# Retention loop of a decoder step: rows fetched a head ahead, rotary products after the values, states on other queues, x chunks one ahead

## The chip, the core and the metric

The kernel runs on one core of a Trainium2 chip. The core has five engines with queues of their own: TensorE (PE, with its weight loads shown apart as PEld), VectorE (DVE), ScalarE (ACT), GpSimd (POOL) and SyncE (SP). An engine takes the instructions of its queue in order; an instruction that has to wait holds up what stands behind it. Transfers between the chip's memory (DRAM) and the on-chip SBUF are issued from the queues of SP, ACT or POOL. The metric is device time in microseconds; lower is better.

## The reference, cut to what matters

One layer of a decoder: half-step SwiGLU, a token mixer of two branches (spatial gating and multi-scale retention), and a second half-step SwiGLU, on 512 prompt tokens and 8 x 8 new tokens (576 columns in all). The change touches the retention branch and the preparation of its input. Per head (8 heads, 128 wide queries and keys, 256 wide values):

```python
def rotary(x, pos):                       # angle per position and per one of 64 frequencies
    x1, x2 = xf[..., :half], xf[..., half:]
    return concatenate([x1 * cos - x2 * sin, x1 * sin + x2 * cos], axis=-1)

def retention_chunk(q, k, v, S, log_gamma):
    scores = einsum('blhd,bshd->bhls', q, k) * decay[None]
    intra = einsum('bhls,bshe->blhe', scores, v)
    inter = einsum('blhd,bhde->blhe', q, S) * q_decay[None, :, :, None]
    S_new = exp(L * log_gamma) * S + einsum('blhd,blhe->bhde', k * k_decay, v)
    return intra + inter, S_new
```

For the prompt the state starts at zero and runs through four chunks of 128 tokens; for the new tokens a state of 128 x 256 for each of 8 sequences and 8 heads is read, used and written back. The result is normalised per head, multiplied with a gate and goes through the projection w_b, whose products are summed over the heads.

## The kernel before, in words

Activations lie transposed in SBUF: 128 channels on the partitions, the 576 tokens along the row, so that "a row" or "a chunk" below is a tile of 128 x 576 in fp32 (288 KB). Each matrix product is made of three products of values split into a high and a low part (hi and lo), so that each weight tile and each operand is cast by ACT (`ACT.copy` to hi) and subtracted by DVE (lo): L150 and L151 for weights, L158 and L159 in `split`.

The program is traced in one order by Python; the tile framework then places the instructions of each engine's queue, also out of the traced order where an instruction isn't ready by its own estimate. Work that should run beside the matrix products is written as generators: `start(gen, delay)` hands one over, each `tick(us)` after some matmuls takes time off its delay and runs it to its next `yield`, and `finish` runs it to its end.

**The stages around the change.** The first FFN ends at about 460 us. Then 21 pairs of projections (q and k per head, gate rows, sigmoid gates) stream through `stream(pair2(w))` (L1236), whose results go to DRAM by POOL's queue (L1129): `qkd` holds q and k of each head, `rgd` the two gate rows of each head. Beside it, the generator `operands_of_values` (L1208) brings the residual x back from DRAM (`x1d`) in eight chunks of 128 channels: it issues the load of a chunk (POOL, L1215), yields for 6 us of ticks, multiplies it with the norm's row (DVE, L1217), shifts and scales it (ACT L1219, DVE L1223), and splits it into X (ACT L1225, DVE L1227). Tiles of 128 x 576 there come from a pool of `SSLOT` = 11 slots.

Then the loop over the heads (L1503 to L1517) begins. Its tiles come from a pool of `NSLOT` = 33 slots, made by `mix_pools` (L1244) after the first 24 matmuls of head 0's values, which also loads the rotary table `rope` and the constants `selI`. Per head:

- `fetch(hd)` (L1266): six loads of the q and the k row on SP: the row itself (L1272, x) and a second copy whose halves change places (L1273 and L1274, y: partitions 64 to 127 to 0 to 63 and back); two loads of gate rows (L1278); then two products on DVE (x with the cosines L1280, y with the signed sines L1281) and a sum on POOL (L1282).
- `values_of(hd)` (L1285): loads of w_in (SP, L139), 4 x 24 matmuls L1295 and 16 matmuls L1308 for the new tokens; copies out of PSUM on ACT (L1301).
- `out_b(hd - 2)` (L1486), twice: w_b's loads, 16 products of 6 matmuls (L447) with their copies on ACT (L1492), and eight stores to `accd`, for head 0 plain stores on SP (L1496), then accumulating stores on POOL (L1498).
- `finish(prev)`, and `core(hd)` (L1317) is started; it runs in pieces beside the values and out_b of the next turn.

For head 0 the values come before the fetch. `core` loads the head's constants `hc` (SP L1321) and the states `S0` of the new tokens in four loads of 256 KB (SP L1325; four buffers, so a load waits for the store of the head before to land), makes the scores (PE L1331, L1338, DVE L1333, L1340), transposes k (L1355, L1369; ACT L1357, L1371), corrects the low parts (DVE L1377, L1381), makes the four prompt states S (PE L1393, DVE L1396 and L1398; store of the last on SP, L1402), the product with S0 (PE L1409), the outputs (L1422 to L1443), the new states (PE L1452, DVE L1456; four stores on SP, L1457), the norm (PE L1467, ACT L1471, DVE L1474 to L1482, POOL L1481) and the split for out_b (`split`).

PSUM has eight banks, all from one pool (`bank()`), so a product that needs a bank waits until some engine has read an older one.

Of the kernel before, what the change touches and what calls it, by code (L numbers as in the profile page):

```python
# [28 lines left out]
EPS = 1e-6  # L29
NT = 5  # L30
SG = 4
NSLOT = 33
NSLOT2 = 7
SSLOT = 11
FSLOT = 12
# [44 lines left out]
def layer_kernel(ctx: ExitStack, tc: tile.TileContext, a):  # L80
# [5 lines left out]
    pp = ctx.enter_context(tc.tile_pool(name="pp", bufs=8, space=PSUM))  # L86
    dr = ctx.enter_context(tc.tile_pool(name="dr", bufs=1, space=DRAM))
    wp = ctx.enter_context(tc.tile_pool(name="wp", bufs=1))
    snp = ctx.enter_context(tc.tile_pool(name="snp", bufs=1))
    places = ExitStack()  # L90

    count = [0]
# [10 lines left out]
        return stack.enter_context(tc.tile_pool(name=nm(name), bufs=1, side=side, reuse_waits="tile"))  # L103

    now["xa"], now["xs1"] = pool(places, "xa"), pool(places, "xs1")

    def slot(shape, dt=F32):

# [23 lines left out]
    def whl(shape):  # L132
        small = len(shape) == 3 and shape[1] == 1
        tag = "whs" if small else "whl"
        return wp.tile([P] + shape, F32R, tag=tag, name=nm(tag), bufs=1 if small else 4)

    def load_raw(src, k0, kc, c0, cols):
        raw = raw4([kc, cols])
# [479 lines left out]

    def snap(ps, t=None):
        if t is None:  # L620
            t = snp.tile([P, H], F32, tag="sn", name=nm("sn"), bufs=3)
        ACT.copy(out=t, in_=ps[:, :H])  # L622
        return t

# [583 lines left out]
    def operands_of_values():  # L1208

        g = a2()  # L1210
        row = slot([P, T])
        POOL.dma_start(out=row, in_=rowd)
        for c in range(KC):
            t = slot([P, T])
            POOL.dma_start(out=t, in_=x1d[:, c])  # L1215
            yield 6.0
            DVE.tensor_tensor(out=t, in0=t, in1=row, op=ALU.mult)  # L1217
# [47 lines left out]

    def fetch(hd):  # L1266

        rope, t = tks["rope"], []
        for i in range(2):
            src = qkd[:, 2 * hd + i]  # L1270
            x, y = slot([P, T]), slot([P, T])
            nc.sync.dma_start(out=x, in_=src)  # L1272
            nc.sync.dma_start(out=y[0:64], in_=src[64:128])  # L1273
            nc.sync.dma_start(out=y[64:128], in_=src[0:64])  # L1274
            t.append((x, y))
        rg = [slot([P, T]) for _ in range(2)]
        for e in range(2):
            nc.sync.dma_start(out=rg[e], in_=rgd[:, 2 * hd + e])  # L1278
        for x, y in t:
            DVE.tensor_tensor(out=x, in0=x, in1=rope[:, 0], op=ALU.mult)  # L1280
            DVE.tensor_tensor(out=y, in0=y, in1=rope[:, 1], op=ALU.mult)  # L1281
            POOL.tensor_tensor(out=x, in0=x, in1=y, op=ALU.add)  # L1282
        return t[0][0], t[1][0], rg

    def values_of(hd):  # L1285
        wv = [load_w(win, 4 * i, 4, RV0 + hd * DV, DV) for i in range(2)]
        rv = []
        for n in range(4):
            ps = bank()
            i = 0  # L1290
            for kk in range(KC):
                wh, wl = (w[:, kk % 4, :] for w in wv[kk // 4])
                xh, xl = (x[:, n * P:(n + 1) * P] for x in X[kk])
                for s, m in ((xh, wh), (xl, wh), (xh, wl)):
                    PE.matmul(ps[:, :DV], lhsT=s, rhs=m, start=i == 0, stop=i == 23)  # L1295
                    i += 1
            if not rts:
                mix_pools()
            if n % 2 == 0:
                rv.append(slot([P, 2, DV]))  # L1300
            ACT.copy(out=rv[n // 2][:, n % 2, :], in_=ps[:, :DV])  # L1301
            tick(24 * 0.109)
        rvs = rts[0].tile([P, DV], F32, tag="rvs", name=nm("rvs"), bufs=2)
        ps = bank()
        i = 0
        for kk in range(KC):
            for w in wv[kk // 4]:
                PE.matmul(ps[:, :DV], lhsT=tks["hs"][:, kk, :], rhs=w[:, kk % 4, :], start=i == 0, stop=i == 15)  # L1308
                i += 1
        sw = half()  # L1310
        ACT.copy(out=sw[0:NS, :DV], in_=ps[NS:P, :DV])
        ACT.copy(out=sw[NS:P, :DV], in_=ps[0:NS, :DV])
        DVE.tensor_tensor(out=rvs, in0=ps[:, :DV], in1=sw[:, :DV], op=ALU.add)
        tick(16 * 0.109)
        return rv, rvs

    def core(hd, q, k, rg, rv, rvs, OB):  # L1317
        rt, selI = rts
        qdS = tks["qdS"]
        hc = rt.tile([P, 338], F32, tag="hc", name=nm("hc"), bufs=2)  # L1320
        nc.sync.dma_start(out=hc, in_=a["hconst"][hd])  # L1321
        S0 = []
        for j in range(4):
            t = rt.tile([P, 2, DV], F32, tag="S0", name=nm("S0"), bufs=4)
            nc.sync.dma_start(out=t, in_=a["state_ret"][0, 2 * j:2 * j + 2, hd].rearrange("b d e -> d b e"))  # L1325
            S0.append(t)

        ps = bank()
        for n in range(4):
# [61 lines left out]
        for n in range(4):  # L1391
# [7 lines left out]
                    out=t, in0=S[-1], scalar=lg[hd] ** P, in1=ps[:, :DV], op0=ALU.mult, op1=ALU.add  # L1399
                )  # L1400
            S.append(t)
        nc.sync.dma_start(out=a["ret_state_prompt"][0, 0, hd], in_=S[3])  # L1402
        yield 4.0

        pi = bank()
# [43 lines left out]
        for j in range(4):  # L1449
            ps = bank()  # L1450
            for i in range(2):
# [5 lines left out]
            nc.sync.dma_start(  # L1457
                out=a["ret_state_sample"][0, 2 * j:2 * j + 2, hd].rearrange("b d e -> d b e"), in_=S0[j]
            )
        yield 4.0  # L1460
# [19 lines left out]
        for e in range(2):  # L1480
            POOL.tensor_tensor(out=o[e], in0=o[e], in1=rg[e], op=ALU.mult)  # L1481
            DVE.tensor_tensor(out=o[e], in0=o[e], in1=r, op=ALU.mult)  # L1482
            split(OB[e][0], OB[e][1], o[e])
        yield 0.0

    def out_b(hd, OB, j):  # L1486
        wb = load_w(a["w_b"][0], 2 * hd, 2, j * 512, 512)
        for c in range(4):
# [4 lines left out]
                tick(cost(2))  # L1493
            dst = accd[:, 4 * j + c, :]
            if hd == 0:
                nc.sync.dma_start(out=dst, in_=t)  # L1496
            else:
                POOL.dma_start(out=dst, in_=t, accum_op=ALU.add)  # L1498


    prev = None
    OBs = []
    for hd in range(HEADS):  # L1503
        if hd == 0:
            rv, rvs = values_of(hd)
            q, k, gates = fetch(hd)
        else:
            q, k, gates = fetch(hd)
            rv, rvs = values_of(hd)
        if hd > 1:  # L1510
            for j in range(2):
                out_b(hd - 2, OBs[hd - 2], j)
        if prev:
            finish(prev)
        OBs.append([])
        prev = core(hd, q, k, gates, rv, rvs, OBs[hd])
        start(prev, 0.5)  # L1517


# [204 lines left out]
        xt2.append(xp.tile([P, 2, T], F32, tag="x", name=nm("x2"), bufs=4))  # L1724
        nc.sync.dma_start(out=xt2[p], in_=x1d[:, 2 * p:2 * p + 2, :])
    xs = [xt2[c // 2][:, c % 2] for c in range(KC)]
    now["xs1"] = pool(ffn2, "xs1")
    now["wraw"] = pool(ffn2, "raw")
    ops.clear()
    now["hl"] = pool(hreg, "hl", "right")  # L1730
# [118 lines left out]
def shape_constants():  # L1849
# [5 lines left out]
    ang = (pos[None, :] * inv[:, None]).astype(f32).astype(np.float64)  # L1855
    rope = np.zeros((P, 2, T), f32)
    rope[0:64, 0], rope[64:128, 0] = np.cos(ang), np.cos(ang)
    rope[0:64, 1], rope[64:128, 1] = -np.sin(ang), np.sin(ang)
    hconst = np.zeros((HEADS, P, 338), f32)
    i = np.arange(P)  # L1860
    j = np.arange(NS)
# [54 lines left out]
```

## Time and profile before

| | us |
|---|---|
| median of three runs | 1746.78 (1738.07 to 1747.7) |
| the profiled execution | 1745.23 |
| its span, first to last instruction | 1743.5 |
| PE busy | 1667.8 (96%) |
| DVE busy | 1132.4 (65%) |
| ACT busy | 789.9 (45%) |
| POOL busy | 276.3 (16%) |
| mean granted PE clock | 0.982 of full |

How to read the rows quoted below. In the timeline a row has start, length, engine, line of the kernel, operation, the tile written and the tiles read, shapes, and how many instructions were merged; in brackets stands how long the engine had been idle before and what released it. "SPq" and "ACTq" are the queues that issue transfers; their instructions do not count as busy. In the table of waits: who waited on which line for whom, total us, times, longest. In the table of stretches: busy time of each engine with the number of instructions, the granted PE clock (1.00 is full), the mean busy share of the 16 DMA engines and the GB/s they moved. In the answers for one line: shortest, median and longest duration in ns, then the starts of the first and the last.

### The profile page before, as it was taken

To read this page: it belongs to the slowest core of one execution; us is meant where nothing else is said; L and a number is where in the kernel's file an instruction comes from. 1 tells how busy PE (TensorE), PEld (TensorE's weight loads), DVE (VectorE), ACT (ScalarE), POOL (GpSimd) and SP (SyncE) were. 2 spreads that over 40 slices of the span, in tenths; PEclk is the share of its full clock that TensorE was granted. 3 is DMA by queue.
4 is the path that set the end of the run, shared out by engine and by line. 5 is a ranking of instruction groups with operands and counts; after the bars stand their busy time and mean duration, and the time that the engine had idled before them with its cause. 6 is when DMAs were issued, how large, how long until landed. Compare 5 with 4: busy or idle time off the path is not lost.

```text
span 1743.5 us, 30978 instructions
## 1 busy us (share of the span) xinstructions
PE 1667.8 (96%) x12324; PEld 1588.9 (91%) x12324; DVE 1132.4 (65%) x1796; ACT 789.9 (45%) x1374; POOL 276.3 (16%) x340
## 2 busy tenths in 40 slices
PE   8999999999999999997988889999999999999997
PEld 4889999999999988987978889889999999999997
DVE  6857847676787766736654556355656958676773
ACT  5533525344655546533444444523335625344454
POOL 0000000001211100013334445103512000000002
PEclk9999999999999999998999999999999999999999
DMA  9443544424366656666676777544951232322331
GB/s 304 139 134 97 149 130 122 133 86 128 104 192 211 210 172 199 201 222 177 209 198 177 191 188 194 135 113 117 275 176 50 72 99 86 92 84 84 93 97 55
DMA packets 305618, 256.77 MB, mean 147 GB/s; under 512 B 14009, under 2 KB 260025, under 8 KB 305474
## 3 DMA queue, kind: packets, MB, share of 16 engines
q1 hardware_dynamic: 290450, 218.82, 41.9%
q0 software_dynamic: 12720, 33.63, 8.5%
q8 instruction: 96, 1.57, 0.4%
q10 hardware_dynamic: 2304, 2.36, 0.4%
q14 instruction: 48, 0.39, 0.1%
HBM read 207.01 MB, written 47.74 MB: 146 GB/s over the span
## 4 chain that ended last, share of the span: by engine, by line
PE 77%; DMA 7%; issue 6%; DVE 5%; ACT 2%; POOL 2%; SPq 1%; POOLq 0%; ACTq 0%; DVEq 0%
PE ps L613 35%; PE ps L447 28%; PE ps L1295 3%; DMA c<-qkd 3%; PE ps L1534 3%; PE ps L269 2%; DMA ada<-in_w_ada_dram 1%; PE ps L1431 1%; PE ps L1308 1%; DMA c<-x1d 1%; DMA wraw<-in_w_down_dram 1%; PE ps L1437 1%; PE ps L1393 1%; DVE whl L641 1%; DMA ut_ret_state_sample_dram<-S 1%
## 5 line engine op out<-in xcount | busy, mean ns | idle before, releaser
L613 PE MATMUL ps<-xa,whl 128*128 128x288 f32 x3000 | 425.6, 296 | 5.2 <-DVE whl L641 2.0
L613 PEld LDWEIGHTS ps<-xa,whl 128*128 128x128 f32 x3000 | 406.4, 188 | 18.0 <-issue 6.7
L613 PE MATMUL ps<-xs,whl 128*128 128x288 f32 x2040 | 296.9, 299 | 6.3 <-ACT sn L622 6.3
L613 PEld LDWEIGHTS ps<-xs,whl 128*128 128x128 f32 x2040 | 280.8, 190 | 19.8 <-ACT sn L622 11.0
L641 DVE TENSOR_TENSOR whl<-wraw,whl 128x1024 fp32r<-128x1024 f32 x192 | 234.7, 1225 | 56.4 <-ACT whl L631 48.8
L631 ACT CAST whl<-wraw 128x1024 fp32r<-128x1024 f32 x192 | 200.2, 1048 | 109.8 <-DVE wraw L755 62.4
L447 PE MATMUL ps<-c,wd 128*128 128x288 f32 x1824 | 245.7, 295 | 0.0
L447 PEld LDWEIGHTS ps<-c,wd 128*128 128x128 f32 x1824 | 242.8, 188 | 2.7 <-issue 1.7
L447 PE MATMUL ps<-c,whl 128*128 128x288 f32 x1368 | 190.3, 296 | 1.4 <-ACT c L158 1.1
L447 PEld LDWEIGHTS ps<-c,whl 128*128 128x128 f32 x1368 | 183.2, 188 | 2.5 <-ACT c L158 1.4
L434 POOL TENSOR_TENSOR x<-x,s 128x64 f32<-128x64 f32 x72 | 35.8, 497 | 823.8 <-DVE s L433 823.7
L428 DVE SCALAR_TENSOR_TENSOR x<-ps,gate,x 128x288 f32<-128x288 f32 (+1 forms) x128 | 61.1, 481 | 117.9 <-PE ps L447 117.9
L622 ACT COPY sn<-ps 128x288 f32<-128x288 f32 x195 | 77.0, 398 | 100.8 <-PE ps L613 99.8
L151 DVE TENSOR_TENSOR whl<-wraw,whl 128x1024 fp32r<-128x1024 f32 x56 | 70.7, 1269 | 78.4 <-ACT whl L150 78.3
L1295 PE MATMUL ps<-whl,xx 128*128 128x256 f32 x768 | 103.7, 297 | 2.1 <-DVE c L1333 2.1
L1295 PEld LDWEIGHTS ps<-whl,xx 128*128 128x128 f32 x768 | 100.2, 205 | 3.2 <-DVE c L1333 2.3
L914 ACT CAST wd<-wraw 128x640 fp32r<-128x640 f32 (+2 forms) x58 | 45.4, 782 | 110.4 <-PE ps L447 101.9
L613 PE MATMUL ps<-xs,whs 128*128 128x288 f32 x480 | 70.7, 295 | 0.0
L631 ACT CAST whs<-wraw 128x512 fp32r<-128x512 f32 x62 | 38.4, 620 | 66.8 <-PE ps L613 58.6
L613 PEld LDWEIGHTS ps<-xs,whs 128*128 128x128 f32 x480 | 66.2, 188 | 0.8 <-issue 0.8
L150 ACT CAST whl<-wraw 128x1024 fp32r<-128x1024 f32 x56 | 58.3, 1048 | 18.1 <-PE ps L1308 6.4
L919 DVE TENSOR_TENSOR wd<-wraw,wd 128x640 fp32r<-128x640 f32 (+2 forms) x58 | 54.1, 933 | 10.4 <-ACT wd L914 10.3
(273 smaller groups left out, 2203.3 us busy)
## 6 DMA issues: line engine op xcount, KB each, us to landing
ada<-in_w_ada_dram SPq DMA_DIRECT2D x56, 512.0 KB
wraw<-in_w_in_dram SPq DMA_DIRECT2D x96, 256.0 KB
wraw<-in_w_gate_dram SPq DMA_DIRECT2D x88, 256.0 KB
wraw<-in_w_up_dram SPq DMA_DIRECT2D x88, 256.0 KB
wraw<-in_w_in_dram SPq DMA_DIRECT2D x32, 512.0 KB
accd<-c POOLq DMA_DIRECT2D x56, 288.0 KB, 7.7
wraw<-in_w_down_dram SPq DMA_DIRECT2D x32, 384.0 KB
wraw<-in_w_down_dram SPq DMA_DIRECT2D x32, 320.0 KB
```

The costliest lines, as they stand in the source:

```text
L150: ACT.copy(out=hi, in_=raw)
L151: (eng or DVE).tensor_tensor(out=lo, in0=raw, in1=hi.bitcast(F32), op=ALU.subtract)
L428: DVE.scalar_tensor_tensor(out=x[:, o:o + w], in0=ps[:, :w], scalar=g[:, c, 0:1], in1=x[:, o:o + w], op0=ALU.mult, op1=ALU.add)
L447: PE.matmul(ps[:, :H], lhsT=s[:, k, c0:c0 + P], rhs=m[:, HALF[h]], start=k == 0 and z == 0, stop=k == kc - 1 and z == 2,)
L613: PE.matmul(ps[:, :H], lhsT=s[:, j * P:(j + 1) * P], rhs=m[:, j, :], start=fresh and j == 0 and z == 0, stop=j == 3 and z == 2, skip_group ...
L622: ACT.copy(out=t, in_=ps[:, :H])
L631: ACT.copy(out=hl[:, 0], in_=src)
L641: DVE.tensor_tensor(out=hl[:, 1], in0=src, in1=hl[:, 0].bitcast(F32), op=ALU.subtract)
L914: ACT.copy(out=hl[:, 0], in_=self.raw[c])
L919: DVE.tensor_tensor(out=lo, in0=self.raw[c], in1=hi.bitcast(F32), op=ALU.subtract)
L1295: PE.matmul(ps[:, :DV], lhsT=s, rhs=m, start=i == 0, stop=i == 23)
L1534: PE.matmul(ps, lhsT=s, rhs=m[:, kx % 2, :], start=kx == 0 and z == 0, stop=kx == KC - 1 and z == len(terms) - 1,)
```

## The change

- **Rows:** `fetch(hd)` only loads: q, k and the two gate rows, four loads on SP, and it is called for head hd + 1 at the top of turn hd (for heads 0 and 1 ahead of the loop's first values). The second copy of q and k with halves changed over is gone.
- **Rotary:** a function `rotary(x)` is called after `values_of(hd)`. It makes y by two DVE products of 64 partitions each, which read one half of x and write the other half of y, multiplies x with the cosines (DVE) and adds (POOL). The table of sines is stored with its sign and halves so that both inputs of a product lie on the same partitions.
- **States:** `hc` and `S0` are loaded by `states(hd, queue)`: for head 0 from SP ahead of the loop, for head hd + 1 from ACT's queue at the end of `core(hd)`. The stores of the prompt state, of S0 and of head 0's out_b go from SP to POOL.
- **Pools:** `mix_pools` runs ahead of the loop. Two small pools (`sn`, `whs`) are closed during the mixer and opened again for the second FFN; `NSLOT` goes from 33 to 36.
- **x chunks:** `operands_of_values` asks for chunk c + 1 before it works on chunk c, with 14 us more of ticks at its start.

```diff
@@ NSLOT, pools
-NSLOT = 33
+NSLOT = 36
...
-    snp = ctx.enter_context(tc.tile_pool(name="snp", bufs=1))
...
+    now["sn"], now["whs"] = pool(places, "sn"), pool(places, "whs")
...
@@ operands_of_values
-        for c in range(KC):
-            t = slot([P, T])
-            POOL.dma_start(out=t, in_=x1d[:, c])
+        come = []
+        for c in range(KC + 1):
+            if c < KC:
+                come.append(slot([P, T]))
+                POOL.dma_start(out=come[c], in_=x1d[:, c])
             yield 6.0
+            if c == 0:
+                yield 14.0
+                continue
+            c, t = c - 1, come[c - 1]
@@ fetch, rotary, states
-        rope, t = tks["rope"], []
-        for i in range(2):
-            src = qkd[:, 2 * hd + i]
-            x, y = slot([P, T]), slot([P, T])
-            nc.sync.dma_start(out=x, in_=src)
-            nc.sync.dma_start(out=y[0:64], in_=src[64:128])
-            nc.sync.dma_start(out=y[64:128], in_=src[0:64])
-            t.append((x, y))
-        rg = [slot([P, T]) for _ in range(2)]
-        for e in range(2):
-            nc.sync.dma_start(out=rg[e], in_=rgd[:, 2 * hd + e])
-        for x, y in t:
-            DVE.tensor_tensor(out=x, in0=x, in1=rope[:, 0], op=ALU.mult)
-            DVE.tensor_tensor(out=y, in0=y, in1=rope[:, 1], op=ALU.mult)
-            POOL.tensor_tensor(out=x, in0=x, in1=y, op=ALU.add)
-        return t[0][0], t[1][0], rg
+        t = [slot([P, T]) for _ in range(4)]
+        for i in range(4):
+            nc.sync.dma_start(out=t[i], in_=qkd[:, 2 * hd + i] if i < 2 else rgd[:, 2 * hd + i - 2])
+        return t
+
+    def rotary(x):
+        rope, y = tks["rope"], slot([P, T])
+        DVE.tensor_tensor(out=y[0:64], in0=x[64:128], in1=rope[64:128, 1], op=ALU.mult)
+        DVE.tensor_tensor(out=y[64:128], in0=x[0:64], in1=rope[0:64, 1], op=ALU.mult)
+        DVE.tensor_tensor(out=x, in0=x, in1=rope[:, 0], op=ALU.mult)
+        POOL.tensor_tensor(out=x, in0=x, in1=y, op=ALU.add)
+
+    def states(hd, queue):
+        rt = rts[0]
+        hc = rt.tile([P, 338], F32, tag="hc", name=nm("hc"), bufs=2)
+        queue.dma_start(out=hc, in_=a["hconst"][hd])
+        S0 = []
+        for j in range(4):
+            t = rt.tile([P, 2, DV], F32, tag="S0", name=nm("S0"), bufs=4)
+            queue.dma_start(out=t, in_=a["state_ret"][0, 2 * j:2 * j + 2, hd].rearrange("b d e -> d b e"))
+            S0.append(t)
+        tks["states"] = hc, S0
 
@@ values_of
-            if not rts:
-                mix_pools()
@@ core
-        hc = rt.tile([P, 338], F32, tag="hc", name=nm("hc"), bufs=2)
-        nc.sync.dma_start(out=hc, in_=a["hconst"][hd])
-        S0 = []
-        for j in range(4):
-            t = rt.tile([P, 2, DV], F32, tag="S0", name=nm("S0"), bufs=4)
-            nc.sync.dma_start(out=t, in_=a["state_ret"][0, 2 * j:2 * j + 2, hd].rearrange("b d e -> d b e"))
-            S0.append(t)
+        hc, S0 = tks["states"]
 
...
-        nc.sync.dma_start(out=a["ret_state_prompt"][0, 0, hd], in_=S[3])
+        POOL.dma_start(out=a["ret_state_prompt"][0, 0, hd], in_=S[3])
...
-            nc.sync.dma_start(
+            POOL.dma_start(
                 out=a["ret_state_sample"][0, 2 * j:2 * j + 2, hd].rearrange("b d e -> d b e"), in_=S0[j]
             )
...
+        if hd + 1 < HEADS:
+            states(hd + 1, nc.scalar)
         yield 0.0
@@ out_b, for hd == 0
-                nc.sync.dma_start(out=dst, in_=t)
+                POOL.dma_start(out=dst, in_=t)
@@ the loop
-    prev = None
-    OBs = []
+    mix_pools()
+    states(0, nc.sync)
+    coming, prev, OBs = fetch(0), None, []
     for hd in range(HEADS):
-        if hd == 0:
-            rv, rvs = values_of(hd)
-            q, k, gates = fetch(hd)
-        else:
-            q, k, gates = fetch(hd)
-            rv, rvs = values_of(hd)
+        mine = coming
+        coming = hd + 1 < HEADS and fetch(hd + 1)
+        rv, rvs = values_of(hd)
+        for x in mine[:2]:
+            rotary(x)
         if hd > 1:
             for j in range(2):
                 out_b(hd - 2, OBs[hd - 2], j)
         if prev:
             finish(prev)
         OBs.append([])
-        prev = core(hd, q, k, gates, rv, rvs, OBs[hd])
+        prev = core(hd, mine[0], mine[1], mine[2:], rv, rvs, OBs[hd])
         start(prev, 0.5)
 
 
...
-    now["xs1"] = pool(ffn2, "xs1")
+    now["xs1"], now["sn"], now["whs"] = pool(ffn2, "xs1"), pool(ffn2, "sn"), pool(ffn2, "whs")
@@ the table of sines
-    rope[0:64, 1], rope[64:128, 1] = -np.sin(ang), np.sin(ang)
+    rope[0:64, 1], rope[64:128, 1] = np.sin(ang), -np.sin(ang)
```

More of the change, by code (lines that the diff above doesn't have):

```diff
@@ L134, in whl @@
         tag = "whs" if small else "whl"
-        return wp.tile([P] + shape, F32R, tag=tag, name=nm(tag), bufs=1 if small else 4)
+        return (now["whs"] if small else wp).tile([P] + shape, F32R, tag=tag, name=nm(tag), bufs=1 if small else 4)
     def load_raw(src, k0, kc, c0, cols):
@@ L620, in snap @@
         if t is None:
-            t = snp.tile([P, H], F32, tag="sn", name=nm("sn"), bufs=3)
+            t = now["sn"].tile([P, H], F32, tag="sn", name=nm("sn"), bufs=3)
         ACT.copy(out=t, in_=ps[:, :H])
```

## The prediction, made before the changed kernel was run

> **What bounds the kernel now.** I read the page first, then the table of stretches cut at the same instruction (the first L1467 matmul) of successive heads, then PE's waits, then the timeline where PE stands still, on every engine and on SP's queue.
>
> ```profile
> span 1743.5 us, 30978 instructions
> ...
> PE 1667.8 (96%) x12324; PEld 1588.9 (91%) x12324; DVE 1132.4 (65%) x1796; ACT 789.9 (45%) x1374; POOL 276.3 (16%) x340
> ```
>
> PE is busy for 96% of the span, so only its 76 us of idle time and its slow-clock time can be won. The profiled execution took 1745.23 us, its span and 1.7 us around it; the median of the three runs shown is 1746.78, so both stand for the same kernel. The stage that the change touches is the loop over heads:
>
> ```profile
> core 0: us, PE busy (x) PEld busy (x) DVE busy (x) ACT busy (x) POOL busy (x), PEclk, DMA share, GB/s
> 851.40:890.52 39.12, 37.02 (x314) 35.66 (x313) 24.30 (x33) 18.80 (x42) 14.21 (x13) 1.00 0.67 205
> 890.52:937.98 47.46, 39.45 (x314) 37.85 (x313) 23.54 (x33) 18.81 (x42) 18.45 (x18) 0.89 0.70 183
> 937.98:983.03 45.05, 39.12 (x314) 37.51 (x313) 24.39 (x33) 18.80 (x42) 18.57 (x18) 0.92 0.74 192
> 983.03:1027.37 44.34, 38.90 (x314) 37.30 (x313) 24.22 (x33) 18.80 (x42) 18.57 (x18) 0.92 0.75 196
> 1027.37:1072.23 44.86, 38.44 (x314) 36.84 (x313) 24.25 (x33) 18.81 (x42) 18.57 (x18) 0.92 0.75 190
> sum 220.83, PE 192.92 PEld 185.15 DVE 120.69 ACT 94.03 POOL 88.37; mean PE 38.58 PEld 37.03 DVE 24.14 ACT 18.81 POOL 17.67
> ```
>
> Each row holds the same 314 matmuls. At full granted clock they take PE 37.02 us (first row); the last four periods take 44 to 47 us, through gaps and through a granted clock of 0.89 to 0.92. Five periods at 37.02 would be 185.1 where 220.8 are spent: 35.7 us too many. One gap in full (timeline, all engines):
>
> ```profile
> 934.20 3.53 SPq L1457 DMA_DIRECT2D ut_ret_state_sample_dram<-S  x4
> 937.83 7.29 SPq L1325 DMA_DIRECT2D S<-in_state_ret_dram  x4
> ...
> 945.79 0.62 SPq L1272 DMA_DIRECT2D c<-qkd  x1
> ...
> 949.61 0.70 ACT L1357 ACTIVATE c<-ps,hc 128x512 f32<-128x512 f32 x1
> 951.53 1.46 PE L1393 MATMUL ps<-c,c 128*128 128x256 f32 x6
> 957.28 0.76 DVE L1280 TENSOR_TENSOR c<-c,rope 128x576 f32<-128x576 f32 x1 [8.88 <-DMA c<-qkd]
> 958.05 0.72 DVE L1377 SCALAR_TENSOR_TENSOR h<-ps,hc,h 32x128 fp32r<-32x128 f32 x2
> 958.92 1.19 PE L1393 MATMUL ps<-c,c 128*128 128x256 f32 x2 [5.93 <-DVE h L1377]
> 959.55 7.72 PE L1295 MATMUL ps<-whl,xx 128*128 128x256 f32 x48
> ```
> ```profile
> 829.86 5.80 PE L1295 MATMUL ps<-whl,xx 128*128 128x256 f32 x48
> ```
> ```profile
> PE ps L1393 <- DVE h L1377: 25.8, 4, 8.0
> ...
> SPq L1325 <- DMA ut_ret_state_sample_dram<-S: 22.8, 16, 3.4
> ```
>
> Read it upwards. PE waits for L1377, which has to leave a PSUM bank; L1377 is queued on DVE behind the rotary product L1280; L1280 waits for the q row; and that row was issued at 945.79 because SP stood for 7.29 us in front of four state loads, each waiting for the state store ahead of it to land. The rows are not slow, they are issued late, in order. The same 48 matmuls then take 7.72 us instead of 5.80: the clock has dropped. PE's table has four such waits, 25.8 us; with the 2.1 us of idle time in the first period and the lower clock they make the 35.7.
>
> **The change, part by part.** *Rows a head ahead, states off SP.* The loads of S0 and of the head's constants go to ACT, the stores of S0 and S to POOL, and the rows of head hd+1 are asked for before the values of head hd. SP then has nothing that waits for a store, and a row has some 37 us for a trip that took 11.5 (945.79 to 957.28). Both causes of L1280's wait go: I count the whole 35.7 us. What is late next is ACT (below).
>
> *Rotary.* Two copies of 144 KB per row go; three DVE products per row take the place of two, 6 instead of 4 a head.
>
> ```profile
> L1280 DVE TENSOR_TENSOR c<-c,rope x16: 740/759/1883, 781.4 to 1049.8; 128x576 f32<-128x576 f32 x16
> ...
> 1004.28 1.41 POOL L1282 TENSOR_TENSOR c<-c,c 128x576 f32<-128x576 f32 x1 [10.19 <-DVE c L1281]
> 1004.58 1.72 DVE L1280 TENSOR_TENSOR c<-c,rope 128x576 f32<-128x576 f32 x1 [0.44 <-DMA c<-qkd]
> ```
>
> The trace has no product that moves halves across partitions; by these rows two more cost 1.5 us (2 x 0.76) to 3.8 us (2 x 1.88) of DVE a head, and I take the low end, as most of the sixteen are near it. In an undisturbed period DVE is busy 24.3 of 39.1 us; its 14.8 idle us hide either end, so I count nothing. Without that cover, right ahead of L1377, it would be up to 3.8 us a head. The long product ran beside a GpSimd one. The Trainium skill (SBUF — State Buffer, Who interferes with whom) says why: a Vector instruction with two SBUF inputs and a GpSimd instruction that reads SBUF shut each other out for a whole instruction. That speaks against two more such products; by it the sum moves towards 3.8 us of hidden DVE time and stays as it is.
>
> *GpSimd's queue* gets five stores more a head (and, for head 0 alone, the eight accumulator stores).
>
> ```profile
> L1498 POOL DMA_DIRECT2D accd<-c x56: 854/872/2403, 886.7 to 1228.6; - x56
> ...
> L1129 POOL DMA_DIRECT2D qkd<-c x16: 539/539/544, 491.7 to 584.7; - x16
> ```
>
> That is 2.7 us (5 x 0.54) to 12.0 us (5 x 2.40); I take 4.4 (5 x 0.87), the accumulating stores of the same loop. POOL is busy 18.6 of 45 us, so it is hidden. A store waits for L1456, with the accumulating stores and the gate product L1481 behind it, which nobody needs before the next head. Counted: nothing; uncovered, 4.4 us a head would delay L1282 and so L1331.
>
> *ScalarE's queue* gets five loads a head, and the four of S0 wait there for the stores of S0. This is the new wait.
>
> ```profile
> L1185 ACTq DMA_DIRECT2D x1d<-x x16: 326/327/1033, 422.3 to 457.3; - x16
> ...
> 943.23 1.35 ACT L158 CAST c<-c 128x576 fp32r<-128x576 f32 x2 [3.12 <-DVE c L1482]
> ```
>
> Issuing costs 1.6 us a head (5 x 0.33). Behind the loads stand out_b's copies L1492, which free PSUM banks, and L1357, whose result L1393 needs. L1357 ended at 950.31 and L1393 began at 951.53: 1.2 us of slack, less than the issue time. The wait for the stores is between nothing (they have landed when ACT comes) and the 7.29 us in which SP stood for the same loads; 3.12 us of it can fall into the time that ACT waits for L1482 anyway. Per head PE loses between 0 and 7.3 us. I take 1.0, near the low end, because ACT comes to these loads only after most of that landing time has gone by; seven heads hand over a state: 7 us lost.
>
> *x chunks a chunk ahead* in the stage before:
>
> ```profile
> 628.19 0.55 POOL L1215 DMA_DIRECT2D c<-x1d  x1
> ...
> 633.00 3.36 PE L613 MATMUL ps<-xa,whl 128*128 128x288 f32 x24
> ...
> 635.41 0.76 DVE L1217 TENSOR_TENSOR c<-c,c 128x576 f32<-128x576 f32 x1 [5.10 <-DMA c<-x1d]
> 639.76 6.13 PE L613 MATMUL ps<-xs,whl 128*128 128x288 f32 x24 [3.40 <-ACT sn L622]
> ...
> 668.22 0.66 PE L281 MATMUL ps<-ident,ada 128*128 128x128 f32 x4 [0.72 <-ACT ada L275]
> 670.23 3.45 PE L613 MATMUL ps<-xs,whl 128*128 128x288 f32 x24 [1.35 <-ACT sn L622]
> ...
> 499.03 2.94 PE L613 MATMUL ps<-xa,whl 128*128 128x288 f32 x20 [1.15 <-DVE whl L641]
> ```
>
> DVE stands 5.10 us for a chunk asked for 7 us before; PE then idles 3.40 us and does 24 matmuls in 6.13 instead of 3.36 us: 6.2 us. The other two chunks that were late cost 0.72 + 1.35 and 1.15 us. Sum 9.4 us, all of it gone, since the next chunk is then asked for some 24 us ahead. The bound below is nothing, should the eleven slots not free one in time.
>
> *The first head.*
>
> ```profile
> 789.51 2.08 PE L1331 MATMUL ps<-c,c 128*128 128x128 f32 x8 [6.01 <-POOL c L1282]
> 821.67 1.05 PE L1331 MATMUL ps<-c,c 128*128 128x128 f32 x8
> ```
>
> Here rows can't be a head ahead. The wait of 6.01 us and the slower matmuls (2.08 for 1.05) bound the gain at 7.0 us; below nothing it can go by the 1.5 us of products. I take 2.5, since the four half copies no longer run ahead of the gates and k. The pools that move their place (three more slots) cost nothing: their tiles are used long after.
>
> **Sum:** 1745.2 - 35.7 - 9.4 - 2.5 + 7.0 = 1704.6, say **1705 us**.
>
> **The rivals.** *ACT waits longer* (chance 0.17). If the loads meet the stores' full landing time, 7.3 - 3.1 - 1.2 = 3.0 us a head are lost, 21 instead of 7: 1719 us. For it: the 22.8 us that SP waited on stores; against: ACT gets there later than SP did.
>
> *The DMA engines are the bound* (0.13).
>
> ```profile
> q1 hardware_dynamic: 21262, 28.57, 44.9%
> q0 software_dynamic: 4608, 9.44, 27.2%
> ...
> c<-qkd SPq DMA_DIRECT2D x20, 144.0 KB
> ```
>
> These are the rows for 860 to 1060 us, 4.5 heads. The two queues keep 16 engines busy for 72.1% of 200 us, 32.3 us a head; the half copies (2.95 of q1's 28.57 MB) are 2.1 of these, so 30.2 us stay. If the engines can't be filled further than the 0.74 of the four late periods, a period is 41 us, five are 205: 15.8 us gained instead of 35.7, with nothing more for ACT: 1745.2 - 15.8 - 9.4 - 2.5 = 1717.5. The Trainium skill (DMA: Bandwidth & Descriptors, Issuing engines are not separate DMA queues) says as much: queues of several engines end on the same 16 DMA engines and save only issue time. Against it: at 0.67 in the first period 205 GB/s were moved without a stall, and what held SP was a wait, not the issue.
>
> *The change doesn't do what it says* (0.10). Four rows more are held for a head with three slots more. If SP finds no free slot, the rows come as late as now, and only the chunks count: 1745.2 - 9.4 = 1736.
>
> *Slower* (0.10). ACT stands for the stores not in its own waits but ahead of the copies that free banks: PE idles the 7.3 us, and the clock drops as now (7.72 for 5.80, 1.9 us): 9.2 us at seven heads, 64 us against the 47.6 gained: 1762 us. It decides from 47.6 / 7 = 6.8 us lost a head.
>
> **How the numbers follow.** The forecast has 0.50. The range of 1692 to 1738 holds it (with ACT at nothing and the first head at its bound: 1693), both middle rivals, and the case of the missing slots; it leaves out the slower rival and a gain beyond the counted. A measurement of this kernel tells about 0.5%, 8.7 us, from no change: below 1738.0 is faster. All of the first three and most of the fourth lie there: 0.86 faster, 0.04 within, 0.10 slower.
>
> **What would show it.** Right: in the loop over heads, no wait of L1393 for L1377, the granted clock at 1.00, periods near 38 us, rows issued a period ahead, and DVE never waiting for a row or an x chunk. ACT's table shows the price: loads of S0 that wait for stores, and PE waiting for L1357 or for banks. It is wrong if DVE still waits for rows (slots, or products queued ahead of their rows), if the periods stay above 41 us with the DMA share near 1 (DMA), or if PE waits for ACT several us a head.

## The result, and the profile after

The changed kernel takes 1742.71 us (median of 12 runs, 1739.53 to 1745.92), the kernel before 1740.82 us (12 runs, 1733.48 to 1747.7): a ratio of 1.0005 with a 95% interval of 0.9988 to 1.0022. There is no difference that can be measured, where 1705 us were forecast.

The page of the changed kernel, its first lines:

```profile
span 1739.5 us, 30929 instructions
...
PE 1672.1 (96%) x12324; PEld 1590.3 (91%) x12324; DVE 1167.2 (67%) x1812; ACT 789.9 (45%) x1374; POOL 311.4 (18%) x388
```

DVE has 35 us more work than before and POOL 35 us more; PE is as busy as it was. Line numbers have moved by a few: the values are L1307 now, k·q L1335, the state matmuls L1397, the product with S0 L1413, the new states L1456 (PE) and L1460 (DVE), the norm L1471 (PE) and L1475 (ACT), the rotary products L1281 to L1283 with the sum L1284 (POOL).

The table of stretches of the changed kernel, cut at the first L1471 matmul of successive heads as before:

```profile
core 0: us, PE busy (x) PEld busy (x) DVE busy (x) ACT busy (x) POOL busy (x), PEclk, DMA share, GB/s
851.75:892.64 40.89, 39.14 (x315) 37.30 (x313) 28.76 (x36) 18.83 (x41) 19.38 (x24) 0.96 0.58 190
...
936.48:980.17 43.69, 39.77 (x314) 37.40 (x313) 29.59 (x36) 18.82 (x41) 22.20 (x24) 0.96 0.73 185
...
sum 212.49, PE 197.42 PEld 186.80 DVE 148.68 ACT 94.08 POOL 108.55; mean PE 39.48 PEld 37.36 DVE 29.74 ACT 18.82 POOL 21.71
```

Five periods take 212.5 us instead of 220.8: 8.3 us of the 35.7 are won. The first period, undisturbed before (39.12 us), is now 40.89 us. DVE has 5.6 us more work a head (29.74 against 24.14), although only two products were added. PE's longest waits between 757 and 1100 us:

```profile
PE ps L1335 <- POOL c L1284: 7.8, 1, 7.8
PE ps L1471 <- DVE c L159: 7.5, 6, 1.4
PE ps L1471 <- ACT c L158: 6.5, 1, 6.5
PE ps L447 <- DVE S L1460: 4.9, 6, 0.8
PE ps L1413 <- DMA S<-in_state_ret_dram: 4.0, 5, 1.2
```

The old wait (L1393 for L1377, 25.8 us) is gone. The waits for the first head's sum (L1284) and, once, for L158 have grown, from 6.0 and 3.2 us; those for L159, for L1460 and for S0 are new. PE now stops at another point of the period: at the norm (L1471) and at the bank that L1460 has to read (L447). One such stop, on DVE's timeline and then on PE's, both of the changed kernel:

```profile
969.82 0.75 DVE L1281 TENSOR_TENSOR c<-c,rope 64x576 f32<-64x576 f32 x1
970.58 1.87 DVE L1282 TENSOR_TENSOR c<-c,rope 64x576 f32<-64x576 f32 x1
972.48 0.75 DVE L1281 TENSOR_TENSOR c<-c,rope 64x576 f32<-64x576 f32 x1
973.26 0.76 DVE L1283 TENSOR_TENSOR c<-c,rope 128x576 f32<-128x576 f32 x1
974.05 0.75 DVE L1282 TENSOR_TENSOR c<-c,rope 64x576 f32<-64x576 f32 x1
974.84 1.87 DVE L1449 TENSOR_TENSOR c<-c,c 128x576 f32<-128x576 f32 x1
976.63 1.99 DVE L1283 TENSOR_TENSOR c<-c,rope 128x576 f32<-128x576 f32 x1
978.54 0.67 DVE L1460 SCALAR_TENSOR_TENSOR S<-S,ps 128x512 f32<-128x512 f32 x1
979.14 2.63 DVE L159 TENSOR_TENSOR c<-c,c 128x576 fp32r<-128x576 f32 x1
```
```profile
974.15 1.11 PE L1456 MATMUL ps<-c,c 128*128 128x256 f32 x8
975.10 3.35 PE L447 MATMUL ps<-c,whl 128*128 128x288 f32 x24
979.27 1.06 PE L447 MATMUL ps<-c,whl 128*128 128x288 f32 x6 [0.82 <-DVE S L1460]
980.17 0.29 PE L1471 MATMUL ps<-c,onesr 128*128 128x288 f32 x1
981.83 0.40 PE L1471 MATMUL ps<-c,onesr 128*128 128x288 f32 x1 [1.37 <-DVE c L159]
```

The six products of the next head stand on DVE ahead of L1460 and L159, five of them ahead of L1449 too, and this head's norm needs all three. L1460 starts 4.4 us after the first of the matmuls that it follows (978.54 against 974.15; before the change it was 0.4 us). PE runs out of banks, then out of operands. In the same period DVE had stood idle for 9.3 us:

```profile
966.61 1.23 DVE L151 TENSOR_TENSOR whl<-wraw,whl 128x1024 fp32r<-128x1024 f32 x1 [9.33 <-ACT whl L150]
```

So the idle time was there, at another place in the queue than the products. At their place DVE's timeline of before shows a gap of 3.5 us:

```profile
884.74 0.76 DVE L1445 TENSOR_TENSOR c<-c,c 128x576 f32<-128x576 f32 x1 [3.52 <-ACT c L1443]
886.03 0.69 DVE L1456 SCALAR_TENSOR_TENSOR S<-S,ps 128x512 f32<-128x512 f32 x1 [0.53 <-PE ps L1452]
886.63 0.78 DVE L159 TENSOR_TENSOR c<-c,c 128x576 fp32r<-128x576 f32 x1
```

The six products take 6.9 us there (the rows above, two of them stretched to 1.87 and 1.99 us), and L1449 and L159 are stretched as well. GpSimd's timeline of the same stretch shows what runs beside the stretched rows:

```profile
970.20 1.63 POOL L1485 TENSOR_TENSOR c<-c,c 128x576 f32<-128x576 f32 x1 [12.01 <-ACT c L1447]
974.11 1.99 POOL L1284 TENSOR_TENSOR c<-c,c 128x576 f32<-128x576 f32 x1 [2.27 <-DVE c L1283]
976.06 1.95 POOL L1485 TENSOR_TENSOR c<-c,c 128x576 f32<-128x576 f32 x1
...
979.11 2.03 POOL L1284 TENSOR_TENSOR c<-c,c 128x576 f32<-128x576 f32 x1
```

L1282 and L1283 are stretched beside this head's gate products (L1485), L1449 and L159 beside the rotary sums (L1284). An estimate from these rows: at 0.76 us each, L1282, L1449 and L1283 would be 3.5 us shorter, of the 4.0 us by which L1460 starts later than before; and L159, at 0.78 instead of 2.63 us, would be 1.9 us shorter, more than PE's stop of 1.37 us. By this estimate the products delay the norm mostly through what runs beside them at this place, and less by their own 4.6 us. No run takes the two apart, since every edit below that moves the products moves their sums too.

The span, cut at three points, says where the 4.0 us between the two profiled spans (1743.5 and 1739.5) come from. The first values start at 761.10 instead of 767.32 (6.2 us won). The norm of the second head starts at 851.75 instead of 851.40 (the first two heads lose 6.6). Five periods later it starts at 1064.24 instead of 1072.23 (8.3 won), and the next stage at 1094.42 instead of 1098.53 (the last head loses 3.9). The profiled execution of before (1745.23) also lay 4.4 us above the median of its twelve runs, and that of the changed kernel (1741.51) 1.2 us below its own; that is why the medians show nothing of these 4.0 us.

### The profile page after: what moved, and what is told of

Same layout as the page of the kernel before. It is cut to its first block, busy times and chain, and to the rows that moved or that the text cites. A ratio compares the mean times of both kernels' runs of the same rounds, so it can differ in the third digit from the quotient of the medians.

```text
span 1739.5 us, 30929 instructions
## 1 busy us (share of the span) xinstructions
PE 1672.1 (96%) x12324; PEld 1590.3 (91%) x12324; DVE 1167.2 (67%) x1812; ACT 789.9 (45%) x1374; POOL 311.4 (18%) x388
## 3 DMA queue, kind: packets, MB, share of 16 engines
q8 instruction: 96, 1.57, 0.4%
## 4 chain that ended last, share of the span: by engine, by line
PE 77%; DMA 7%; DVE 6%; issue 6%; ACT 2%; POOL 1%; SPq 0%; POOLq 0%; DVEq 0%; ACTq 0%
PE ps L613 35%; PE ps L447 29%; DMA S<-in_state_ret_dram 3%; PE ps L1540 3%; PE ps L1307 3%; PE ps L269 2%; DMA ada<-in_w_ada_dram 1%; DVE c L159 1%; PE ps L1318 1%; PE ps L1435 1%; DMA xa<-in_w_ada_dram 1%; DVE S L1460 1%; DMA wraw<-in_w_down_dram 1%; DVE whl L641 1%; ACT whl L631 1%
## 5 line engine op out<-in xcount | busy, mean ns | idle before, releaser
L447 PE MATMUL ps<-c,wd 128*128 128x288 f32 x1824 | 245.5, 295 | 0.0
L447 PEld LDWEIGHTS ps<-c,wd 128*128 128x128 f32 x1824 | 242.8, 188 | 2.5 <-issue 1.7
L447 PE MATMUL ps<-c,whl 128*128 128x288 f32 x1368 | 198.6, 304 | 7.9 <-DVE S L1460 4.9
L447 PEld LDWEIGHTS ps<-c,whl 128*128 128x128 f32 x1368 | 190.2, 195 | 10.6 <-DVE S L1460 6.3
L1307 PE MATMUL ps<-whl,xx 128*128 128x256 f32 x768 | 97.1, 286 | 0.0
L1307 PEld LDWEIGHTS ps<-whl,xx 128*128 128x128 f32 x768 | 93.8, 193 | 0.4
L1498 ACT COPY c<-ps 128x288 f32<-128x288 f32 x128 | 45.4, 406 | 47.8 <-PE ps L447 26.0
```

The costliest lines, as they stand in the source:

```text
L447: PE.matmul(ps[:, :H], lhsT=s[:, k, c0:c0 + P], rhs=m[:, HALF[h]], start=k == 0 and z == 0, stop=k == kc - 1 and z == 2,)
L1498: ACT.copy(out=t[:, HALF[h]], in_=ps[:, :H])
```

## The experiments

Theory 1: the products are at the wrong place in DVE's queue. Theory 2: they are too much work wherever they stand, slowed by GpSimd beside them. Theory 3: the loads on ScalarE's queue and the stores on GpSimd's are the cause. Each time below is a median; the ratio is to the runs of the kernel before on the same chip. The medians of the kernel before go from 1739.78 to 1742.26 us between chips, so small differences are read from the ratios.

**Products inside the values.**

```diff
             tick(24 * 0.109)
+            if n == 2:
+                for x in rows:
+                    rotary(x)
         rvs = rts[0].tile([P, DV], F32, tag="rvs", name=nm("rvs"), bufs=2)
...
-        rv, rvs = values_of(hd)
-        for x in mine[:2]:
-            rotary(x)
+        rv, rvs = values_of(hd, mine[:2])
```

> Only the place of the rotary products is changed: the six products and two sums of head hd are issued inside the values of head hd, after the third group of 24 matmuls, where DVE stands idle for some 9 us in each period of the changed kernel (957.3 to 966.6), and no longer behind the values, right ahead of the sum of squares, the state update and the norm of the head before. Theory 1 (the place on DVE is the cause): PE's waits for DVE ahead of the norm (0.83 + 1.32 + 0.20 us a head) and the matmuls at a clock of 0.54 behind them (7.24 for 5.74 us, 1.5) go, some 3.9 us in five periods, 3.6 us at the last head and some 8 us at the first: about 31 us, 1712 us (1705 to 1722). Theory 2 (six products beside GpSimd's sums are too much work wherever they stand): the waits come back at another place, 1735 to 1745 us. Theory 3 (the loads and stores on ScalarE's and GpSimd's queues are the cause): 1738 to 1745 us.

Measured: 1717.17 us, ratio 0.987 (0.9843 to 0.9897). Theory 1 holds and theories 2 and 3 fall as the main cause: the same six products, moved some 13 us forward in the queue together with their two sums, give back some 24 us (0.987 against 1.0005). PE's waits of this kernel between 755 and 1110 us, the three longest:

```profile
PE ps L1338 <- POOL c L1284: 7.1, 1, 7.1
PE ps L447 <- DVE c L1483: 5.2, 5, 1.1
PE ps L1400 <- ACT c L1364: 4.0, 1, 4.0
```

What is left is the first head (7.1 us), and something new: L1483 is the norm's second step, and on DVE's timeline the step before it (L1481) waits 6.46 us for ScalarE's root (L1478), which stands behind a load of S0.

**No rotary position at all.** Edit: the two lines `for x in mine[:2]: rotary(x)` are taken out.

> The changed kernel with the rotary position left out: q and k go into the core as they were fetched, so that no product and no sum of it is on DVE or GpSimd. Theory 1: like the kernel with the products inside the values, or 1 to 4 us less, since there they cost nothing: 1705 to 1715 us. Theory 2: 20 us or more below the kernel with the moved products. Theory 3: little changes, 1735 to 1743 us.

Measured: 1709.78 us, ratio 0.9816 (0.9793 to 0.984). That is 7.4 us below the products inside the values, and the wait of 7.1 us at the first head is the one that this kernel lacks. So inside the values the products of the other seven heads cost next to nothing. Theory 2, that they cost wherever they stand, is out; what it says of GpSimd beside them is seen above at the one place.

**States on SP again**, with the products left behind the values.

```diff
-            states(hd + 1, nc.scalar)
+            states(hd + 1, nc.sync)
...
-        POOL.dma_start(out=a["ret_state_prompt"][0, 0, hd], in_=S[3])
+        nc.sync.dma_start(out=a["ret_state_prompt"][0, 0, hd], in_=S[3])
...
-            POOL.dma_start(
+            nc.sync.dma_start(
                 out=a["ret_state_sample"]...
```

> The changed kernel with the state loads and the state stores on SP's queue, as before the change; rows a head ahead and the rotary products behind the values stay. Theories 1 and 2: the waits of PE for DVE are as in the changed kernel; SP stands some 7 us a head for the stores again, but the rows were asked for a head ahead, so that it costs little: 1738 to 1748 us. Theory 3: ScalarE's wait at the loads and GpSimd's five stores are gone, below 1728 us.

Measured: 1736.7 us, ratio 0.9972 (0.9953 to 0.9991). It is 6 us less than the changed kernel, just outside what theories 1 and 2 gave it and far from theory 3's 1728. The waits for L159 and L1460 are as in the changed kernel (7.7 and 4.9 us in six heads); the wait of L1413 for S0 (4.0 us) is gone. The queues are a second, smaller cost.

**The x chunks alone**, put into the kernel before.

> The kernel before with the x chunks asked for a chunk ahead, and nothing else of the change. If the step is worth what its stalls show, and nothing later gives it back: 6.2 us (the one long stall, by which the first values begin earlier in the changed kernel's trace) to 9.4 us less than before, 1731 to 1735 us. If the time is given back in the loop over heads, whose waits hang on transfers and not on PE: 1738 to 1742 us.

Measured: 1735.77 us, ratio 0.997 (0.9949 to 0.9991): 4.0 us less, within an interval of 1.6 to 9. It lies between the two expectations, and is taken up again below.

**Products inside the values and states on SP.** Edit: that of the first and of the third experiment together.

> The products inside the values (as in the first experiment, 1717.2 us), and the state loads and stores on SP's queue as before the change. In the first experiment's trace ScalarE stands at the loads of S0 until the stores have landed, ahead of the reciprocal root of the norm: PE waits 5.2 us in five heads for the norm's second step, 4.0 + 2.0 us at the second head. Theory A (ScalarE's standing is what is left of the queues' cost): these waits go, 1717 - 5.2 - 4.0 - 2.0 = 1706 us (1702 to 1711). Theory B (SP standing for the same stores delays weights or rows instead, as it did before): 1714 to 1722 us.

Measured: 1706.41 us, ratio 0.9802 (0.9776 to 0.9829), as theory A had it. The waits for L1483 are gone. What ScalarE did, from its timeline in the kernel with the products inside the values and the loads on its queue:

```profile
927.08 0.37 ACTq L1293 DMA_DIRECT2D S<-in_state_ret_dram  x1
927.49 0.40 ACT L1501 COPY c<-ps 128x288 f32<-128x288 f32 x1 [4.03 <-DMA ut_ret_state_sample_dram<-S]
...
927.79 0.90 ACT L1478 ACTIVATE r<-ps,epsT 128x288 f32<-128x288 f32 x2
```

The load of S0 has a place ahead of a copy that frees a bank and ahead of the norm's root. It waits 4.03 us until the store of the head before has landed, and both wait with it.

**The first head's products ahead of its values.**

```diff
+        if hd == 0:
+            for x in mine[:2]:
+                rotary(x)
+        rv, rvs = values_of(hd, mine[:2] if hd else [])
```

> The products inside the values, but those of head 0 ahead of the values of head 0. In the first experiment PE waits 7.1 us for the first head's rotated rows, although they were asked for at 759.3: its products are queued on DVE behind a weight product that waits 10.7 us for its slot (775.1). Theory A (the place in DVE's queue again): the rows have landed by some 768 us, the products end before PE needs them, and the 7.1 us and the slower matmuls behind them (2.08 for 1.05 us) go: 1717.2 - 8 = 1709 us. Theory B (the rows land late, or the time is given back at the next wait for ScalarE): 1714 to 1718 us.

Measured: 1712.52 us, ratio 0.9838 (0.981 to 0.9867): 4.7 us less than with all products inside the values, between the two theories. The trace, of the fastest of the six runs, shows a part of each: PE's wait for the first head's sum falls from 7.1 to 1.8 us, but the wait for L1364 at the second head stays at 4.1 us.

**Both.** Edit: states on SP, products inside the values, those of head 0 ahead of them.

> Products inside the values, those of head 0 ahead of them, states on SP. If both gains are independent: 1717 - 11 - 8 = 1698 us (1694 to 1704). If they share one wait (the second head's): 1703 to 1708 us.

Measured: 1697.49 us (1693.04 to 1702.71), ratio 0.9752 (0.9724 to 0.9779). Both gains add up. This version beats both kernels, by 2.5% the one before. Its stretches, from the fastest of its six runs (1693.04 us):

```profile
835.31:872.15 36.84, 36.84 (x314) 35.67 (x313) 24.80 (x35) 18.80 (x42) 16.49 (x18) 1.00 0.64 206
872.15:908.99 36.84, 36.84 (x314) 35.67 (x313) 25.40 (x35) 18.80 (x42) 19.11 (x18) 1.00 0.83 220
```

Length and PE's busy time are the same number in every row (the three left out are 36.84 too), and the clock is 1.00: in these five periods of the profiled run PE never stops. DVE has 25.4 us of work, 4.3 less than in the changed kernel with the same six products. SP still stands 7.53 us in front of the four loads of S0:

```profile
871.97 7.53 SPq L1293 DMA_DIRECT2D S<-in_state_ret_dram  x4
```

It costs nothing there: the rows behind it are those of the next head, and PE waits for no weight in these periods.

**Products ahead of the values**, where the kernel before had them, with rows a head ahead and the rest of the change as it is.

```diff
+        for x in mine[:2]:
+            rotary(x)
         rv, rvs = values_of(hd)
-        for x in mine[:2]:
-            rotary(x)
```

> The changed kernel with the products of each head ahead of its values, where the kernel before had them; the rows still come a head ahead. It tells whether the late rows alone made the wait of 25.8 us. Theory 1 (any place on the way of the norm, the masks or L1381 costs; here some 4.6 us of products stand ahead of them at the period's start): PE waits 2 to 4 us a head for DVE ahead of the state matmuls, 1718 to 1738 us. Rival (the rows were all of it, and DVE has room there): no such wait, the periods as short as with the products inside the values, 1708 to 1718 us.

Measured: 1716.9 us, ratio 0.9859 (0.9832 to 0.9885). The rival holds and theory 1 was too wide: there is no wait of L1397 for DVE. Late rows alone had made the wait of 25.8 us, and the old place would have done. Of the three places tried, only the one behind the values costs so much. (PE waits 8.5 us in five heads for ScalarE's L1361 here. The longest of these waits, 4.3 us, comes after ScalarE's stop at the loads of S0. In the other four, of 1.05 us each, L1361 stands on ScalarE behind a copy of the values, L1311, which itself waits for PE; that is not the loads' doing.)

**Which queue?** Two kernels beside the one with both edits: stores on GpSimd with loads on SP, and loads on ScalarE with stores on SP.

> The kernel with products inside the values, head 0's ahead of them and states on SP (1697.5 us), but with the stores of S0 and S on GpSimd's queue, the loads on SP. Theory A (ScalarE standing at the loads is what the queues cost; the stores cost nothing on GpSimd, whose 4.4 us a head were counted as hidden): within 3 us of 1697.5. Rival (GpSimd's stores, queued behind its sums and gate products, go out late, so that the loads land late): 1702 to 1710 us.

Measured: 1700.79 us, ratio 0.9755 (0.9731 to 0.9778). The median lies 3.3 us above the other's, just outside theory A's 3 us; the ratio is the same as 0.9752. No cost of the stores on GpSimd can be measured, within some 6 us.

> The same kernel with the stores on SP and only the loads of S0 and the constants on ScalarE's queue. Theory A: ScalarE stands some 4 us a head for the stores to land, ahead of a copy that frees a bank and of the norm's root; PE waits 1.0 us a head in five heads and some 4 us at the second head, and does slower matmuls behind it: 1704 to 1711 us. Rival (the loads were late only because GpSimd's stores were): within 3 us of 1697.5.

Measured: 1720.61 us, ratio 0.9876 (0.9852 to 0.99), some 22 us more by the ratios, and outside both expectations. Theory A has the right queue and too small a size. The timelines of SP and ScalarE in this kernel show a longer stop:

```profile
875.14 2.22 SPq L1464 DMA_DIRECT2D ut_ret_state_sample_dram<-S  x3
...
879.40 8.86 ACTq L1293 DMA_DIRECT2D S<-in_state_ret_dram  x3
888.30 0.40 ACT L1501 COPY c<-ps 128x288 f32<-128x288 f32 x1 [8.81 <-DMA wraw<-in_w_in_dram]
```

The last store is issued by 877.36 and the last load leaves ScalarE's queue at 888.26, 10.9 us later. In the kernel that differs from this one only by having the stores on GpSimd (1712.52 us) it is 6.4 us at the same place (875.91 to 882.35). In five successive heads of each kernel it is 8.4 to 10.9 us with the stores on SP and 6.4 us each time with the stores on GpSimd. So the stores' queue sets how long the loads hold ScalarE. The bracket names the landing of a weight load as what ended the stop shown; for three of the other four it names the landing of a store. That period takes 42.60 us at a granted clock of 0.92; others of this kernel take 38.11. Why the stores let the loads go later from SP's queue stays open.

**Both edits without the x chunks.** Edit: the lines of the x chunks as before the change.

> The same kernel (1697.5 us) with the x chunks fetched as before the change. By itself the chunk step gave 4.0 us (1.6 to 9) where 9.4 were counted; here no wait stands behind it that could give time back. If the step is worth its stalls: 6 to 9 us more, 1703.5 to 1707 us. If the 4.0 us are its size: 1701 to 1702 us.

Measured: 1701.26 us, ratio 0.9764 (0.9742 to 0.9785), 3.8 us more than with them by the medians and 2 us by the ratios (0.9764 against 0.9752). This lies within the noise, so it agrees with the 4.0 us of the first measurement but does not confirm them. PE's stops in this stage, in the kernel with both edits and without the chunks, and then in the changed kernel:

```profile
640.82 4.98 PE L613 MATMUL ps<-xs,whl 128*128 128x288 f32 x24 [2.98 <-ACT sn L622]
667.98 0.66 PE L281 MATMUL ps<-ident,ada 128*128 128x128 f32 x4 [0.68 <-ACT ada L275]
669.99 3.46 PE L613 MATMUL ps<-xs,whl 128*128 128x288 f32 x24 [1.36 <-ACT sn L622]
```
```profile
663.25 0.66 PE L281 MATMUL ps<-ident,ada 128*128 128x128 f32 x4 [0.48 <-ACT ada L275]
665.26 4.97 PE L613 MATMUL ps<-xs,whl 128*128 128x288 f32 x24 [1.35 <-ACT sn L622]
```

The long stop goes with the chunks. The two behind it (0.7 and 1.35 us) are there with the chunks ahead too. In the changed kernel the 24 matmuls behind the second take 4.97 us instead of 3.46, so that 1.5 us are lost again there.

## Why the prediction was wrong, point by point

**The step that failed** is the cost of the rotary products: "In an undisturbed period DVE is busy 24.3 of 39.1 us; its 14.8 idle us hide either end, so I count nothing." The 14.8 us are a sum over the period. The products stand at one place of an in-order queue, and of the idle time only what lies there can hide them. The trace of before had shown that place too: 3.5 us ahead of L1445, and from there on L1445, L1456 and L159 with hardly a gap. The prediction did bound the price of a missing cover, but "right ahead of L1377", the old place, and not at the new one. What the runs showed in its place: room of 3.5 us for products that took 6.9 us there, with L1449 and L159 stretched by what GpSimd ran beside them. Moving the products and their sums alone gives some 24 us back.

**Their duration** was bounded at 1.5 to 3.8 us more a head and came to 5.6 us of DVE time, since neighbours grew as well. The answers for L159, in the changed kernel and in the one with both edits:

```profile
L159 DVE TENSOR_TENSOR c<-c,c x16: 750/758/2683, 850.7 to 1063.2; 128x576 fp32r<-128x576 f32 x16
```
```profile
L159 DVE TENSOR_TENSOR c<-c,c x15: 749/761/772, 841.3 to 1015.6; 128x576 fp32r<-128x576 f32 x15
```

The same instruction takes 2.68 us at worst where the rotary sums of GpSimd run beside it, and never over 0.77 us where they run elsewhere. The prediction had a rule of the Trainium skill (SBUF — State Buffer, Who interferes with whom) in hand, that such a pair shuts each other out, and the trace agrees. It was applied to the products and not to what stands behind them.

**Late rows, 35.7 us:** the cause was right, and the size came out once the other stops were gone. Five periods without stops are 184.2 us (5 x 36.84), 36.6 less than before, with rows ahead, products inside the values and states on SP together. With rows ahead and the products at their old place they are 196.2 us, 24.7 less than before, with stops for ScalarE still in them. In the changed kernel it is 8.3 us, since the new wait stands in its place. One of its periods (936.48 to 980.17) is 43.69 us: 36.84, 2.34 us of waits for DVE (0.82 + 1.32 + 0.20), 1.57 us for S0 (0.34 + 1.23), and 2.9 us of slower matmuls behind these stops.

**ScalarE's queue, 7.0 us:** the mechanism was right (loads that wait for stores, ahead of what frees banks), and the size was low. Taking states off the two queues gives 6 us in the changed kernel, some 11 with the products inside the values and 15 with the first head mended too. Since the stores on GpSimd cost nothing that can be measured when the loads are on SP, this is the loads on ScalarE's queue. What stood behind them was not L1357 alone, as counted, but the copies out of PSUM and the norm's root.

**GpSimd's five stores, nothing:** not contradicted (0.9755 against 0.9752, known to some 6 us).

**x chunks, 9.4 us:** about 4 (1.6 to 9), measured alone. The long stall was one, and its size differs between runs (6.2 us in one profile, 2.98 + 1.5 in another). The stalls of 2.07 and 1.15 us were put down to chunks, though the rows quoted for them name ScalarE's `sn` and `ada` and a weight product, and no chunk.

**The first head, 2.5 us won:** instead 6.6 us were lost in the first heads. The products of head 0 were behind a weight product that waits for its slot, so that rows asked for early were used late (776.03), and the norm of head 0 came late like all others.

**The base:** 1745.2, the profiled execution, was 4.4 us above the median of twelve runs.

**The rivals.** That the DMA engines are the bound is out: periods of 36.84 us run at a share of 0.83. That the change doesn't do what it says is out: neither DVE nor PE waits for a row in the loop. A slower kernel did not come. ScalarE's longer wait was there, but not as the main loss. The case that came, a new wait for DVE in place of the old, was not among the rivals.

## What to carry to other kernels

Idle time of an engine is no cover by itself: look for the gap at the very place in the in-order queue where the new instructions will stand, and name the instruction behind them and who waits for it. When data come earlier, the work on them can be put into the widest gap of its engine; put behind the work of the same turn, it delays the end of the turn before. Look also at what GpSimd runs beside that place: here it more than doubled single products. A load that has to wait for a store belongs on a queue with nothing urgent behind it.

## What the runs showed of the hardware

Stops far shorter than 6 us cost clock too, but not each time. PE of the changed kernel around one norm, and at its waits for S0 in the same period:

```profile
core 0: us, PE busy (x), PEclk, DMA share, GB/s
...
935.50:938.70 3.20, 1.62 (x9) 1.00 1.05 125
938.70:942.00 3.30, 3.30 (x15) 0.54 0.92 272
...
961.00:964.20 3.20, 1.62 (x34) 1.00 0.58 216
964.20:968.00 3.80, 3.80 (x33) 1.00 0.00 0
```

Around the norm PE was still busy half of 3.2 us, in pieces, and then worked 3.3 us at a granted clock of 0.54, so that 42 matmuls took 7.24 us instead of 5.74. At the waits for S0 it was busy the same 1.62 of 3.20 us, and the clock stayed at 1.00. The same stop of 1.35 us was followed by 24 matmuls in 4.97 us in the changed kernel and in 3.46 us in the one with both edits and without the chunks. Stops of 1.0 us a head (products inside the values) left the clock at 1.00. The Trainium skill (TensorE: Matmul & The Clock Gate, Part 1: The HAM clock gate) tells of a half rate after an idle window of some 3.4 us; around the norm the clock fell though PE was busy for half of that time. What decides between the two cases no run here shows.

A product on 64 partitions that moves its half across costs as much as a whole one in place: L1281 and L1282 on 64 partitions take 0.75 us, L1283 on 128 takes 0.76 where nothing stretches it.
